# Remainders of the w_in and w_out weights from a DMA that adds, with deeper rings and another order

## The chip, the cores and the metric

The kernel runs on one core of a Trainium2 chip, in one launch. The metric is the device time of that launch in microseconds (us). The core has a matrix engine (TensorE, in the profile PE), a vector engine (VectorE, DVE), a scalar engine with tables (ScalarE, ACT), a general engine (GpSimd, POOL), a queue engine that here only issues DMAs (SyncE, SP), and 16 DMA engines, all of which can work on one transfer. Each engine takes its instructions in the order in which they stand in its queue.

## The reference

All arithmetic is float32. The first block is two layers of a transformer with modulation from a condition vector; the second block is two further layers with other mixers.

```python
def first_block(...):                      # DEPTH = 2; x: 512 tokens, h = ctx: 256 tokens, D_MODEL = 1024
    for l in range(DEPTH):
        mod = jnp.split(sc @ w_mod[l] + b_mod[l], 6, axis=-1)
        ...
        pc = hn @ w_in[l]                  # last layer: keys and values of the context only
        xn = rms_norm(x, g_norm1[l]) * (1 + scale1) + shift1
        p = xn @ w_in[l]
        ...
        attn = attend_query_blocks(q, ...)
        x_new = mixers_and_ffn(x, p, attn, ...)
        ...

def mixers_and_ffn(...):
    four = fourier_mixer(p[..., OFF_F:OFF_C], w_f)
    conv = conv_module(p[..., OFF_C:OFF_P], dw_w, dw_b, ln_g, ln_b, w_pw)   # 31 taps per channel
    pool = pool_mixer(p[..., OFF_P:], w_pl, pl_scale)                       # windows of 2, 4, 8, 16 tokens
    mix = jnp.concatenate([attn, four, conv, pool], axis=-1) @ w_o
    x = x + gate1 * mix
    xn = rms_norm(x, g2) * (1 + scale2) + shift2
    return x + gate2 * swiglu(xn, w_fi, w_fo)

def second_block(x, ...):
    for layer in range(DEPTH):
        u = rms_norm_2(h, pre_norm[layer])
        ...                                # layer 0: retention and a short convolution; layer 1: causal latent attention
        h = h + rms_norm_2(y, post_norm[layer])
```

`w_in` of the first block has 1536 columns, `w_out` (here `w_o`) is 1024 x 1024, the hidden width of the FFN is 2816.

## The kernel before

A float32 product is made of three matmuls with rounded operands (`mm3`, from line 1162): each weight w is split on the chip into a rounded part `wh` and a remainder `wl` = w - `wh`, each activation into a rounded part and a remainder, and the product is wh x xh + wh x xl + wl x xh. The split of a weight is `weights()` (line 1144): a tile `raw` of 128 x 1024 (512 KB) is loaded by a DMA on SyncE's queue, rounded into `wh` (a CAST on ScalarE or VectorE), and subtracted into `wl` (a TENSOR_TENSOR on VectorE). The three tiles stand in rings: four `raw`, three `wh`, three `wl`. A `raw` tile is free when the subtraction has read it; a `wh` and a `wl` when TensorE has. The activations lie transposed, features on the partitions, 512 tokens of x and 256 tokens of the context beside each other on the free axis.

The stages, in the order of the span: the norm and the first modulation (to about 40 us); the product with w_in in twelve blocks of 128 columns (`WIN_ORDER`, line 67: a and g of the convolution's gate, k, q, v, the pooling and Fourier inputs), between which the mixers of layer 0 run (to about 250 us); the product with w_out (to about 360); the FFN of layer 0 (to about 960); the same for layer 1 (mixers 960 to 1100, w_out to 1185, FFN to about 1560); then the two layers of the second block. In the mixing stages VectorE makes the convolution's taps (`cy` and `cz`, one multiply and add for each of 31 taps, `conv_taps`, line 1302), attention's row sums, and the weight remainders; ScalarE makes exponentials, copies and roundings; GpSimd has the additions of the pooling mixer alone (`pool_task`, line 1367, tiles `ps`). The modulation vectors (`md`) are matmuls on `raw` tiles too in layer 0's mixing stage (`mod_block`, line 1252), and on tiles `mraw` of their own later. The out products take each of the eight blocks of `w_out` once for every 256 tokens: 24 loads in layer 0, 16 in layer 1; in layer 0 and in layer 1 together 26 weights of w_in are loaded.

What sets the order: the whole program is recorded first (`Rec`), and a planner (`Rec.order`, line 748) gives every operation an engine and a place in that engine's queue. It works with a cost for each operation (`cost`, from line 582), penalties for engines (`PEN_*`), an order of steps (`STEPS`), offsets of priority for each mixer (`SHIFTS`) and the depths of the rings. `issue` (line 985) then writes the queues out, so all instructions have one line in the profile, L1001; tiles are told apart by their names. `wi` is the product with w_in, `wo` the one with w_out, `fa`, `fg` and `fo` the FFN, `y` and the like the second block.

Of the kernel before, what the change touches and what calls it, by code (L numbers as in the profile page):

```python
# [69 lines left out]
CFG = {0: {'CONV_AUX': 8,  # L70
     'LATE': -49000.0,
     'LATEM': 26000.0,
# [8 lines left out]
     'PEN_PE': (0, 150, None),  # L81
# [16 lines left out]
 1: {'CONV_AUX': 6,  # L98
# [4 lines left out]
     'PEN_CP': (0, 0, None),  # L103
     'PEN_CZ': (0, 0, None),
     'PEN_PE': (0, 0, None),
# [18 lines left out]
     'PEN_RND': (0, None, None),  # L124
     'PEN_SQ': (None, 0, None),
# [8 lines left out]
     'backlog': 0,  # L134
     'table_slack': 504.2099999999999,
     'urgent': 11068.417919999998},
 3: {'PEN_ADD': (0, None),
     'PEN_AFF': (0, 0, None),
     'PEN_CP': (0, 0, None),
# [15 lines left out]
     'backlog': 0,  # L155
     'table_slack': 338.9702987999999,
     'urgent': 86776.39649279998}}
SHIFTS = {'mla': 10000.0,
 'ret': 12000.0,
 (0, 'c', 'attn'): 7000.0,  # L160
 (0, 'c', 'conv'): 39000.0,
 (0, 'c', 'four'): 16000.0,
 (0, 'c', 'pool'): 43000.0,
 (0, 'c', 'taps'): -92000.0,
# [2111 lines left out]
```

## Time and profile before

| | |
|---|---|
| time, median of 3 runs | 2245.21 us (2242.07 to 2246.84) |
| profiled execution, its time | 2242.23 us |
| its span, first to last instruction | 2240.2 us |
| TensorE busy | 2134.7 us, 95% |
| VectorE busy | 1418.0 us, 63% |
| ScalarE busy | 866.7 us, 39% |
| GpSimd busy | 22.2 us, 1% |
| bytes moved by DMA | 258.44 MB |
| mean granted TensorE clock | 0.98 |

Busy times count compute instructions; an engine that issues a DMA is not counted as busy. The granted clock is the mean over a stretch of what TensorE was given, as a share of its full 2.4 GHz; its lower level is 1.2 GHz. The releaser of a wait is the instruction that a waiting engine's semaphore was last set by.

### The profile page before, as it was taken

How to read it: one execution, taken by the hardware profiler on the slowest of the kernel's cores; microseconds unless marked ns; L12 is line 12 of the kernel's file. 1: busy time of each engine (PE TensorE's matmuls, PEld its weight loads, DVE VectorE, ACT ScalarE, POOL GpSimd, SP SyncE). 2: the span in 40 equal slices, each digit the busy share in tenths (PEclk: the TensorE clock that was granted, in tenths of full speed). 3: DMA queues.
4: the chain of work that ended last, by engine and by line, in shares of the span. 5: the costliest groups of instructions: out<-in, count | busy, mean ns of one | idle time of the engine just before them, and what ended most of it. 6: DMA issues, size and time to landing. Idle time of an engine off the chain costs nothing.

```text
span 2240.2 us, 32559 instructions
## 1 busy us (share of the span) xinstructions
PE 2134.7 (95%) x12922; PEld 1845.7 (82%) x12922; DVE 1418.0 (63%) x2671; ACT 866.7 (39%) x1646; POOL 22.2 (1%) x35
## 2 busy tenths in 40 slices
PE   7799999999999999888899999999999999999997
PEld 3477799888888888777798888888888888989887
DVE  6998886332232232899984333459775685787996
ACT  6457754111212111664852212215341341435662
POOL 0001000000000000000100000000000000000000
PEclk9799999999999999998999999999999999999998
DMA  8225464222331423422043232335323224543223
GB/s 306 98 98 181 161 217 137 76 98 67 125 101 60 148 78 120 145 89 90 20 142 95 96 110 94 113 117 162 104 85 99 90 89 121 166 139 113 66 77 123
DMA packets 87176, 258.44 MB, mean 115 GB/s; under 512 B 10480, under 2 KB 18160, under 8 KB 87024
## 3 DMA queue, kind: packets, MB, share of 16 engines
q1 hardware_dynamic: 87024, 256.36, 35.7%
q8 instruction: 101, 1.65, 0.3%
q14 instruction: 51, 0.42, 0.1%
HBM read 249.24 MB, written 2.10 MB: 112 GB/s over the span
## 4 chain that ended last, share of the span: by engine, by line
PE 77%; DVE 14%; ACT 4%; DMA 2%; issue 2%; SPq 1%; DVEq 0%; ACTq 0%
PE fa L1001 14%; PE fg L1001 14%; PE fo L1001 13%; PE y L1001 5%; PE wi L1001 5%; PE wo L1001 4%; PE gt L1001 2%; PE egc L1001 2%; PE md L1001 2%; DVE wl L1001 2%; PE ecb L1001 2%; PE ecx L1001 2%; PE ecc L1001 2%; PE egr L1001 2%; DVE cy L1001 1%
## 5 line engine op out<-in xcount | busy, mean ns | idle before, releaser
L1001 DVE TENSOR_TENSOR wl<-raw,wh 128x1024 fp32r<-128x1024 f32 (+5 forms) x387 | 434.6, 1125 | 41.4 <-ACT wh L1001 28.9
L1001 ACT CAST wh<-raw 128x1024 fp32r<-128x1024 f32 (+4 forms) x224 | 216.7, 970 | 417.4 <-PE fo L1001 197.4
L1001 DVE CAST wh<-raw 128x1024 fp32r<-128x1024 f32 (+4 forms) x163 | 105.3, 646 | 211.8 <-PE fa L1001 73.7
L1001 DVE TENSOR_TENSOR ft<-ft,fg 128x256 f32<-128x256 f32 (+1 forms) x66 | 39.4, 598 | 270.7 <-PE fg L1001 270.7
L1001 PE MATMUL fo<-hh,wl 128*128 128x512 f32 (+1 forms) x448 | 156.5, 349 | 6.7 <-DVE wl L1001 6.7
L1001 PE MATMUL fo<-hh,wh 128*128 128x512 f32 (+1 forms) x448 | 157.8, 352 | 0.0
L1001 PE MATMUL fo<-hl,wh 128*128 128x512 f32 (+1 forms) x448 | 157.2, 351 | 0.0
L1001 PE MATMUL fa<-yxh,wh 128*128 128x512 f32 (+1 forms) x384 | 144.9, 377 | 0.0
L1001 PE MATMUL fg<-yxh,wh 128*128 128x512 f32 (+1 forms) x384 | 144.4, 376 | 0.0
L1001 PE MATMUL fa<-yxl,wh 128*128 128x512 f32 (+1 forms) x384 | 143.9, 375 | 0.2 <-DVE yxl L1001 0.2
L1001 PE MATMUL fg<-yxl,wh 128*128 128x512 f32 (+1 forms) x384 | 143.9, 375 | 0.0
L1001 PE MATMUL fa<-yxh,wl 128*128 128x512 f32 (+1 forms) x384 | 142.8, 372 | 0.0
L1001 PE MATMUL fg<-yxh,wl 128*128 128x512 f32 (+1 forms) x384 | 142.7, 372 | 0.0
L1001 PE MATMUL y<-mxh,wl 128*128 128x256 f32 x384 | 110.9, 289 | 6.1 <-DVE wl L1001 6.1
L1001 PE MATMUL y<-mxh,wh 128*128 128x256 f32 x384 | 111.8, 291 | 4.7 <-DVE wh L1001 3.3
L1001 PE MATMUL y<-mxl,wh 128*128 128x256 f32 x384 | 110.1, 287 | 0.3 <-DVE mxl L1001 0.3
L1001 ACT ACTIVATE ft<-fa 128x256 f32<-128x256 f32 (+1 forms) x66 | 34.2, 526 | 178.1 <-PE fa L1001 178.1
L1001 PEld LDWEIGHTS fo<-hh,wl 128*128 128x128 f32 x448 | 85.9, 192 | 18.6 <-DVE wl L1001 7.1
L1001 PEld LDWEIGHTS fo<-hh,wh 128*128 128x128 f32 x448 | 85.4, 191 | 8.4 <-issue 1.7
L1001 PE MATMUL wi<-xxh,wh 128*128 128x512 f32 (+1 forms) x240 | 90.5, 377 | 1.6 <-DVE c L1001 0.7
L1001 PE MATMUL wi<-xxh,wl 128*128 128x512 f32 (+1 forms) x240 | 86.5, 360 | 5.3 <-DVE wl L1001 5.3
L1001 PEld LDWEIGHTS fo<-hl,wh 128*128 128x128 f32 x448 | 86.3, 193 | 5.6
(457 smaller groups left out, 5910.5 us busy)
## 6 DMA issues: line engine op xcount, KB each, us to landing
raw<-in_w SPq DMA_DIRECT2D x291, 512.0 KB, 3.6
mraw<-in_wm SPq DMA_DIRECT2D x48, 512.0 KB, 4.8
raw<-in_wm SPq DMA_DIRECT2D x32, 512.0 KB, 4.8
raw<-in_w SPq DMA_DIRECT2D x24, 448.0 KB, 3.4
raw<-in_w SPq DMA_DIRECT2D x32, 320.0 KB, 3.1
mraw<-in_wm SPq DMA_DIRECT2D x32, 256.0 KB, 5.9
raw<-in_w SPq DMA_DIRECT2D x16, 384.0 KB, 3.1
rw<-rt SPq DMA_DIRECT2D x76, 64.0 KB, 2.0
```

Source lines behind the costliest of these rows:

```text
L1001: getattr(engs[o.eng], method)(*[real(a) for a in args], **{k: real(v) for k, v in kw.items()})
```

## The change

For the weights whose key begins with `in` or `out` in layers 0 and 1 of the first block, 26 and 40 of them, the subtraction on VectorE goes. ScalarE instead writes `wl` = -`wh` (an ACTIVATE with Copy and scale -1), and a DMA issued from GpSimd's queue adds the `raw` tile to `wl` in place. `raw` is free when that DMA has landed. The rings become five `raw`, four `wh` and four `wl`; the space comes from a smaller scratch area for DMA descriptors and from tile sizes rounded up to a common size. The planner gets a cost for the new DMA and other settings: some of the penalties, about half of the offsets, the order of steps in both layers of the second block, and WOE and WOS, by which two w_out blocks rather than three are started early, over six rather than seven of the eight inputs.

```diff
-CFG = {0: {'CONV_AUX': 8,
+CFG = {0: {'ADD': ('in', 'out'),
+     'CONV_AUX': 8,
...
-     'WOE': 3,
+     'WOE': 2,
...
-     'WOS': 7,
+     'WOS': 6,
...
- (0, 'c', 'taps'): -92000.0,
+ (0, 'c', 'taps'): -112000.0,
...
+            if eng == "gpsimd":
+                return 1100.0, 1900.0 + (ap.p1 - ap.p0) * ap.n * 4 / 200.0, False
             return max(250.0, (ap.p1 - ap.p0) * ap.n * 4 / 332.0), 1900.0, False
...
-        h = self.pw.tile([P, 1024], F32R, tag="wh", bufs=3, name=self.name("wh"))
-        lo = self.pw.tile([P, 1024], F32R, tag="wl", bufs=3, name=self.name("wl"))
+        h = self.pw.tile([P, 1024], F32R, tag="wh", bufs=4, name=self.name("wh"))
+        lo = self.pw.tile([P, 1024], F32R, tag="wl", bufs=4, name=self.name("wl"))
         self.rnd(h[:, :n], t[:, :n], self.PEN_WH)
-        self.sub_l(lo[:, :n], t[:, :n], h[:, :n], self.PEN_WL)
+        if key[0] in self.ADD:
+            self.nc.scalar.activation(lo[:, :n], h[:, :n].bitcast(F32), AF.Copy, scale=-1.0)
+            self.nc.gpsimd.dma_start(out=lo[:, :n].bitcast(F32), in_=t[:, :n], accum_op=ALU.add)
+        else:
+            self.sub_l(lo[:, :n], t[:, :n], h[:, :n], self.PEN_WL)
...
-    NA, NB, NRAW = 53, 11, 4
+    NA, NB, NRAW = 53, 11, 5
...
-    nc = _bacc.Bacc("TRN2", target_bir_lowering=False, num_devices=1)
+    nc = _bacc.Bacc("TRN2", target_bir_lowering=False, num_devices=1, dynamic_dma_scratch_size=2048)
```

The settings of the second block are tables; in the order of the whole program VectorE has 2593 rows where it had 2650, ScalarE 1624 where it had 1557, GpSimd 100 where it had 34; ScalarE's table loads go from 46 to 49, TensorE's matmuls of 256 columns from 7274 to 7130 and those of 512 from 4746 to 4818.

GpSimd's queue up to the middle of layer 0's mixing stage stands like this in the kernel before, from its first pooling addition (`ps` is a partial window sum, `pb` the padded input):

```order
L1001 TENSOR_TENSOR ps_749<-pb_88 128x527
L1001 TENSOR_TENSOR ps_758<-ps_749 64x512
L1001 TENSOR_TENSOR ps_1802<-pb_96 128x527
L1001 TENSOR_TENSOR ps_1839<-ps_1802 128x525
L1001 TENSOR_TENSOR ps_1802<-ps_1839 128x520
L1001 TENSOR_TENSOR ps_1839<-ps_1802 64x512
```

and like this in the changed kernel, where the first five adds stand ahead of the first pooling addition:

```order
L1004 DMA wl_247<-raw_205 128x1024
L1004 DMA wl_265<-raw_221 128x1024
L1004 DMA wl_641<-raw_516 128x1024
L1004 DMA wl_674<-raw_538 128x1024
L1004 DMA wl_717<-raw_566 128x1024
L1004 ISA
L1004 TENSOR_TENSOR ps_802<-pb_91 128x527
L1004 TENSOR_TENSOR ps_815<-ps_802 64x512
L1004 DMA wl_841<-raw_799 128x1024
L1004 DMA wl_938<-raw_898 128x1024
L1004 DMA wl_1111<-raw_1054 128x1024
L1004 DMA wl_1233<-raw_1173 128x1024
```

The adds are now between the pooling additions, in one queue.

On VectorE the remainders of the k, q and later weights stand behind the taps of the convolution in the kernel before:

```order
L1001 SCALAR_TENSOR_TENSOR cy_702<-cb_693,spt,cy_702 128x505
L1001 SCALAR_TENSOR_TENSOR cy_940<-cb_928,spt,cy_940 128x253
L1001 TENSOR_TENSOR cy_702<-cy_702,cz_751 128x504
L1001 SCALAR_TENSOR_TENSOR cy_940<-cb_928,spt,cy_940 128x252
L1001 TENSOR_REDUCE modT_303<-md_148_974 128x8
L1001 TENSOR_TENSOR wl_1058<-raw_936,wh_983 128x1024
L1001 SCALAR_TENSOR_TENSOR cy_940<-cb_928,spt,cy_940 128x251
L1001 TENSOR_TENSOR modT_303<-modT_303,spt 128x8
L1001 TENSOR_TENSOR wl_1068<-raw_956,wh_994 128x1024
L1001 SCALAR_TENSOR_TENSOR cy_940<-cb_928,spt,cy_940 128x250
```

In the changed kernel these subtractions are gone from VectorE, and ScalarE has the rounding and the negated copy of the first of those weights one behind the other:

```order
L1004 COPY pb_91<-wi_691 128x512
L1004 COPY pb_88<-wi_702 128x256
L1004 COPY ps_815<-ps_802 64x512
L1004 CAST wh_828<-raw_799 128x1024
L1004 ACTIVATE wl_841<-wh_828 128x1024
L1004 CAST wh_928<-raw_898 128x1024
L1004 ACTIVATE wl_938<-wh_928 128x1024
L1004 ACTIVATE sg_942<-wi_874 128x256
L1004 ACTIVATE sg_946<-wi_869 128x512
```

The copy `wl` follows its `wh` directly, ahead of the gate (`sg`) and the taps (`cz`) of the convolution's second 128 channels.

On TensorE the end of the fourth block of the w_in product (`wi`) is followed in the kernel before by two modulation blocks (`md`) and a piece of the context's layer norm (`cm`), and then by the next block:

```order
L1001 MATMUL wi_856<-xc_600,wl_786 128x256
L1001 MATMUL md_922<-raw_574,scp 32x512 x2
L1001 MATMUL md_922<-raw_609,scp 32x512 x2
L1001 MATMUL cm_932<-cy_709,cst 128x256
L1001 MATMUL md_922<-raw_780,scp 32x512 x2
L1001 MATMUL md_922<-raw_796,scp 32x512 x2
L1001 MATMUL md_148_974<-cst,mrow_966 128x128 x4
L1001 MATMUL md_1006<-raw_972,scp 32x512 x2
L1001 MATMUL md_1006<-raw_987,scp 32x512 x2
L1001 MATMUL md_1006<-raw_1016,scp 32x512 x2
L1001 MATMUL md_1006<-raw_1021,scp 32x512 x2
L1001 MATMUL md_155_1041<-cst,mrow_1038 128x128 x4
```

In the changed kernel the next block, with `wh_828` and `wl_841`, comes between the parts of the first modulation block:

```order
L1004 MATMUL wi_874<-xc_601,wl_717 128x256
L1004 MATMUL md_948<-raw_579,scp 32x512 x2
L1004 MATMUL md_948<-raw_596,scp 32x512 x2
L1004 MATMUL wi_959<-xxh_324,wh_828 128x512
L1004 MATMUL wi_959<-xxl_328,wh_828 128x512
L1004 MATMUL wi_959<-xxh_324,wl_841 128x512
L1004 MATMUL md_948<-raw_695,scp 32x512 x2
L1004 MATMUL md_948<-raw_761,scp 32x512 x2
L1004 MATMUL wi_959<-xxh_326,wh_828 128x512
L1004 MATMUL wi_959<-xxl_333,wh_828 128x512
L1004 MATMUL wi_959<-xxh_326,wl_841 128x512
L1004 MATMUL wi_1001<-xc_370,wh_828 128x256 x2
```

The block of the w_in product has moved ahead of most of the modulation work.

## Rows read from the trace of the kernel before

**Rows 1.** The page: busy time, share of the span, instructions of each engine.

```profile
PE 2134.7 (95%) x12922; PEld 1845.7 (82%) x12922; DVE 1418.0 (63%) x2671; ACT 866.7 (39%) x1646; POOL 22.2 (1%) x35
```

**Rows 2.** Windows: length, busy time of each engine, granted clock, DMA share, GB/s.

```profile
30.00:64.00 34.00, 33.31 (x198) 24.20 (x190) 24.12 (x69) 28.32 (x64) 0.66 (x1) 1.00 0.62 225
64.00:120.00 56.00, 41.33 (x182) 28.07 (x182) 54.13 (x108) 17.12 (x30) 1.57 (x2) 0.76 0.36 122
120.00:250.00 130.00, 121.25 (x734) 96.67 (x733) 112.63 (x269) 92.05 (x189) 11.09 (x12) 0.96 0.41 133
250.00:360.00 110.00, 107.42 (x849) 96.21 (x848) 94.76 (x195) 68.06 (x133) 0.00 (x0) 1.00 0.65 215
...
960.00:1100.00 140.00, 120.25 (x727) 104.68 (x727) 131.57 (x242) 92.19 (x163) 7.91 (x6) 0.93 0.20 63
1100.00:1185.00 85.00, 82.16 (x661) 79.80 (x661) 73.22 (x148) 55.32 (x112) 0.00 (x0) 1.00 0.33 102
```

**Rows 3.** Chain of waits, 45 to 130 us: start, length, what.

```profile
67.01 1.15 DVE wl L1001
...
94.03 14.10 DVE cy L1001 x28
...
109.14 1.15 DVE wl L1001
```

**Rows 4.** Timeline, ScalarE: start, length, instruction.

```profile
92.84 1.03 ACT L1001 CAST wh<-raw 128x1024 fp32r<-128x1024 f32 x1
```

**Rows 5.** Timeline, VectorE, the same stretch.

```profile
109.06 1.22 DVE L1001 TENSOR_TENSOR wl<-raw,wh 128x1024 fp32r<-128x1024 f32 x1
```

**Rows 6.** Waits of TensorE, 60 to 120 us: total, times, longest.

```profile
PE wi L1001 <- DVE wl L1001: 5.3, 2, 4.1
PE md L1001 <- DVE cy L1001: 3.7, 1, 3.7
```

**Rows 7.** Waits of TensorE, 960 to 1100 us.

```profile
PE qss L1001 <- ACT qsq L1001: 5.7, 1, 5.7
PE cm L1001 <- DVE cy L1001: 4.8, 2, 3.9
```

**Rows 8.** Tile wl on VectorE, 64 to 250 us: count, durations in ns, first and last.

```profile
L1001 DVE TENSOR_TENSOR wl<-raw,wh x10: 1205/1217/1223, 66.9 to 205.0; 128x1024 fp32r<-128x1024 f32 x10
```

**Rows 9.** The same, 960 to 1060 us.

```profile
L1001 DVE TENSOR_TENSOR wl<-raw,wh x12: 1212/1218/1226, 967.6 to 1050.2; 128x1024 fp32r<-128x1024 f32 x12
```

**Rows 10.** Groups by line and shape, VectorE: busy us, mean ns, idle before.

```profile
L1001 DVE TENSOR_TENSOR wl<-raw,wh 128x1024 fp32r<-128x1024 f32 x291 | 354.7, 1221 | 17.0 <-ACT wh L1001 5.6 <-DVE wh L1001 0.5
```

**Rows 11.** The same, ScalarE.

```profile
L1001 ACT CAST wh<-raw 128x1024 fp32r<-128x1024 f32 x162 | 169.5, 1049 | 280.1 <-PE fo L1001 102.2 <-PE fg L1001 100.5 <-PE wi L1001 15.4
L1001 ACT ACT_TABLE_LOAD x46 | 59.0, 1283 | 2.4 <-PEq L2265 0.7 <-DVE rp L1001 0.6 <-PE r L1001 0.4
```

**Rows 12.** Tile ps on GpSimd, whole span.

```profile
L1001 POOL TENSOR_TENSOR ps<-pb x6: 638/1104/1948, 63.3 to 1077.5; 128x527 f32<-128x527 f32 x4, 128x271 f32<-128x271 f32 x2
```

**Rows 13.** DMA, 250 to 360 us: queue, packets, MB, share; issues, KB, landing.

```profile
q1 hardware_dynamic: 6471, 23.56, 64.1%
...
raw<-in_w SPq DMA_DIRECT2D x29, 512.0 KB, 4.4
```

**Rows 14.** Tile wo on TensorE, 250 to 360 us, one form of three.

```profile
L1001 PE MATMUL wo<-mxh,wh x128: 278/283/467, 298.9 to 357.5; 128*128 128x256 f32 x128
```

**Rows 15.** The page: copies within SBUF, KB each, us to landing.

```profile
rw<-rt SPq DMA_DIRECT2D x76, 64.0 KB, 2.0
```

**Rows 16.** Waits of TensorE, 900 to 960 us.

```profile
PE fo L1001 <- DVE wl L1001: 8.1, 2, 4.3
```

**Rows 17.** Waits of TensorE, 1500 to 2240 us.

```profile
PE y L1001 <- DVE wl L1001: 6.1, 4, 2.2
PE y L1001 <- DVE wh L1001: 3.3, 2, 1.6
PE fo L1001 <- DVE wl L1001: 3.0, 1, 3.0
```

More of the change, by code (lines that the diff above doesn't have):

```diff
@@ L67 @@
 WIN_ORDER = ["a0", "g0", "a1", "g1", "k", "qA", "qB", "v", "p0", "p1", "f0", "f1"]
-CFG = {0: {'CONV_AUX': 8,
+CFG = {0: {'ADD': ('in', 'out'),
+     'CONV_AUX': 8,
      'LATE': -49000.0,
-     'LATEM': 26000.0,
+     'LATEM': 25000.0,
      'LATEW': -3000.0,
@@ L80 @@
      'PEN_CZ': (0, 0, None),
-     'PEN_PE': (0, 150, None),
+     'PEN_PE': (0, 0, None),
      'PEN_RND': (0, None, None),
@@ L97 @@
      'urgent': 3873.946271999999},
- 1: {'CONV_AUX': 6,
+ 1: {'ADD': ('in', 'out'),
+     'CONV_AUX': 6,
      'FOC': 5000.0,
@@ L102 @@
      'PEN_CA': (0, None),
-     'PEN_CP': (0, 0, None),
+     'PEN_CP': (300, 0, None),
      'PEN_CZ': (0, 0, None),
-     'PEN_PE': (0, 0, None),
+     'PEN_PE': (0, 300, None),
      'PEN_RND': (0, 1000, None),
@@ L123 @@
      'PEN_PE': (0, 0, None),
-     'PEN_RND': (0, None, None),
-     'PEN_SQ': (None, 0, None),
+     'PEN_RND': (0, 150, None),
+     'PEN_SQ': (300, 0, None),
      'PEN_SUB': (0, None),
@@ L128 @@
      'PEN_WL': (0, None),
[5 rows of a table removed]
-     'backlog': 0,
-     'table_slack': 504.2099999999999,
-     'urgent': 11068.417919999998},
[5 rows of a table added]
+     'backlog': 1.5,
+     'table_slack': 2722.7339999999995,
+     'urgent': 29884.72838399999},
  3: {'PEN_ADD': (0, None),
-     'PEN_AFF': (0, 0, None),
-     'PEN_CP': (0, 0, None),
+     'PEN_AFF': (0, 300, None),
+     'PEN_CP': (0, 300, None),
      'PEN_PE': (0, 0, None),
@@ L145 @@
      'PEN_WL': (0, None),
[7 rows of a table removed]
[6 rows of a table added]
      'YE': 1,
      'YS': 4,
-     'backlog': 0,
+     'backlog': 0.25,
      'table_slack': 338.9702987999999,
@@ L158 @@
 SHIFTS = {'mla': 10000.0,
- 'ret': 12000.0,
+ 'ret': -8000.0,
  (0, 'c', 'attn'): 7000.0,
- (0, 'c', 'conv'): 39000.0,
- (0, 'c', 'four'): 16000.0,
+ (0, 'c', 'conv'): 42000.0,
+ (0, 'c', 'four'): 11000.0,
  (0, 'c', 'pool'): 43000.0,
- (0, 'c', 'taps'): -92000.0,
+ (0, 'c', 'taps'): -112000.0,
  (0, 'x', 'attn'): -3000.0,
- (0, 'x', 'conv'): 48000.0,
+ (0, 'x', 'conv'): 56000.0,
  (0, 'x', 'four'): 19000.0,
@@ L171 @@
  (1, 'x', 'conv'): 63000.0,
- (1, 'x', 'four'): -6000.0,
- (1, 'x', 'pool'): 84000.0,
+ (1, 'x', 'four'): -3000.0,
+ (1, 'x', 'pool'): 83000.0,
  (1, 'x', 'taps'): 25000.0}
@@ L971, in order @@
                     finish(o, end)
-                    heapq.heappush(events, (end + (o.lat if e == "sync" else 0.0) + FREE, 1, o.idx))
+                    heapq.heappush(events, (end + (o.lat if e in ("sync", "gpsimd") else 0.0) + FREE, 1, o.idx))
                     heapq.heappush(events, (end, 2, -1))
@@ L1018 @@
     PTW = 4
+    ADD = ()
     PEN_RND = (0.0, None, None)
@@ L1097, in W @@
     def W(self, n, nm="w"):
-        return self.A(nm=nm) if n <= 512 else self.pp.tile([P, n], F32, tag="w", bufs=4, name=self.name(nm))
+        return self.A(nm=nm) if n <= 512 else self.pp.tile([P, 544], F32, tag="w", bufs=4, name=self.name(nm))[:, :n]
     def two(self, n, nm, mk=None):
@@ L1874, in first_layer @@
         self.ffn(l, groups, after)
-    NA, NB, NRAW = 53, 11, 4
+    NA, NB, NRAW = 53, 11, 5
     def setup(self):
         nc = self.nc
-        t = self.psm.tile([P, 8, 2], F32, tag="sc", bufs=1, name="sc")
+        t = self.ptop.tile([P, 24], F32, name="sc")[:, :16].rearrange("p (k v) -> p k v", v=2)
         nc.scalar.activation(t, self.S("c").rearrange("p (k v) -> p k v", v=2), AF.Silu)
@@ L2225, in run @@
             nsp = sum(n for _, n in self.sp_at.values())
-            self.spt = pc.tile([P, nsp], F32, name="spt")
+            self.spt = pc.tile([P, nsp + 40], F32, name="spt")[:, :nsp]
             self.scp = pc.tile([P, 8, 32], F32, name="scp")
@@ L2239, in run @@
             self.nph = 0
+            self.ptop = pool("top", bufs=1, side="right")
             self.pm = pool("pm", bufs=4, space=PSUM, reuse_waits="tile")
```

23 rows, old and new, of the table CFG are left out of this document.

## The prediction

> **What bounds the kernel now.** I first read the page: TensorE is busy 95% of the span, VectorE 63%, ScalarE 39%, GpSimd 1% [rows 1]. So the kernel can only get shorter where TensorE idles or runs at its lower clock. I then cut the span into stages with the windows view and looked, in each row, at TensorE's busy time against the length, at which other engine is nearly full, at the granted clock and at the DMA share [rows 2]. 30 to 64 us is full (33.31 of 34). The mixing stage of layer 0, 64 to 250 us, leaves TensorE 14.67 + 8.75 = 23.4 us idle, while VectorE is busy 54.13 + 112.63 = 166.8 of 186 us, 90%. The mixing stage of layer 1, 960 to 1100 us, leaves 19.75 us idle with VectorE at 131.57 of 140, 94%. The stages of the w_out product, 250 to 360 and 1100 to 1185 us, leave only 2.6 and 2.8 us, and the first has the DMA engines at a mean share of 0.65.
>
> Third, the chain of waits in the first mixing stage: a subtract `wl` of 1.15 us releases TensorE at 68.2, a run of convolution taps `cy` of 14.1 us follows at 94.0, and behind it stands another `wl` at 109.14 [rows 3]. The timeline says why: ScalarE had rounded a `wh` at 92.84, yet the subtract that was next starts on VectorE only at 109.06, behind the taps [rows 4, 5]. The waits of TensorE there are 5.3 us on `wl` and 3.7 on `cy` [rows 6]. In layer 1 the longest is on ScalarE's `qsq`, 5.7 us, and then on the taps, 4.8 [rows 7]: VectorE is full, but the last to arrive is not always a weight.
>
> **The change, part by part.** The sum is made against the profiled execution, 2242.2 us; the median of the runs is 2245.2, 3.0 higher.
>
> 1. Subtracts leave VectorE in the mixing stages. Ten subtracts of 128x1024 stand between 64 and 250 us [rows 8], each 1.22 us busy [rows 10] and 1.15 us in the chain [rows 3]. Removed: 10 x 1.15 = 11.5 us of an engine that is 90% full. To that I add part of TensorE's 4.1 us wait at 68.2, which ends with the subtract: behind a DMA that is fed by ScalarE the weight no longer queues with taps. The orders shown above agree: the negated copy stands right behind its rounding on ScalarE, no tap between, and TensorE's next w_in block comes ahead of most of the modulation work. I take 15 us. From below, 0: the taps are then next on VectorE's queue and the same wait is for them. From above 23.4, all of the idle time; at a mean clock of 0.76 and 0.96 [rows 2] another 0.24 x 56 + 0.04 x 130 = 18.6 could come back, if TensorE idled no longer ahead of its slow stretches, so the far bound is 42. In layer 1 twelve leave [rows 9]: 12 x 1.15 = 13.8; since the longest wait there is ScalarE's I take 12, bounds 0 and 19.75 + 0.07 x 140 = 29.6.
>
> 2. What takes their place. Each of the 66 weights (26 of w_in, 40 of w_out) now has a negated copy on ScalarE and a DMA on GpSimd's queue. The copy has the shape of the cast `wh` on ScalarE, 1.05 us [rows 11], together 66 x 1.05 = 69 us. ScalarE is busy 92 of 130 and 92 of 140 us in the mixing stages [rows 2], so the copies lie beside other work, with VectorE as the cover; were it gone, 22 of them (those two stages) cost up to 23 us. The order has three more ACT_TABLE_LOADs, 3 x 1.28 = 3.8 [rows 11]. I take +3, bounds 0 and +27. On GpSimd's queue the adds stand with the additions of the pooling mixer in one order, and the first of these waits for the pooled input: an add behind it waits too, and behind the add the loads of the raw ring on SyncE. One pooling addition is 0.64 to 1.95 us [rows 12], so one that stands ahead of an add and has its input costs it at most 2 us, which is in the bounds.
>
> 3. The w_out stages. Here the subtracts cost nothing (the idle time of the first is 2.6 us with TensorE 98% busy), so the gain is at most 2.6 and what is added can only lose. In 250 to 360 us the DMA engines are busy 64.1% of the time, 70.5 us, for 23.56 MB [rows 13], which makes 0.524 / 23.56 x 70.5 = 1.57 us of all 16 for one weight. 24 adds now come on top. The trace has no such operation. From below: like a load of the same bytes, 24 x 1.57 = 37.7, and 70.5 + 37.7 = 108.2 of 110 us, which just fits. From above: both operands cost as much as a load, 24 x 3.14 = 75.4, 145.9 us of DMA in 110, +36. I take +10, nearer to the first, which it equals in bytes written; the loads ahead of the stage can be brought earlier, but DMA slices that stand idle in between cannot all be filled. The raw ring: one weight of the second half takes TensorE 3.7 us (128 matmuls of each of three forms, 24 in all per weight, so 16 weights, from 298.9 to 357.5 [rows 14]), and five raw tiles cover 18.4 us. A tile is held 4.4 us for the load [rows 13], 1.05 for the cast, 1.05 for the copy, about 1 to 2 for GpSimd and then for the landing of the add, for which the nearest row is a copy within SBUF of 64 KB, 2.0 us [rows 15]; with 1.57 for the bytes 4 us, with twice the bytes 6. That is 11 to 15 us: the ring holds. In layer 1 the share is 0.33 of 85 us = 28, and 16 adds bring 25 to 50: 53 to 78 of 85. I take +2 for the longer way of each first weight, bounds -2.8 and +10.
>
> The Trainium skill speaks against the change here ("Collectives: The Full Stack", section "The bandwidth ceiling: the fold count and why AG ≠ RS ≠ AR"): a DMA that adds reads two sources, and so moves about half of what a copy does. By that rule the add stands at my upper bound, and the sum would be that of case A; no row of before shows an add.
>
> 4. Deeper rings and the new order. Over the rest TensorE waits 8.1 us on `wl` between 900 and 960 us and 6.1, 3.3 and 3.0 us on `wl`, `wh` and `wl` after 1500 [rows 16, 17]: 20.5 us. A fourth `wh`/`wl` and a fifth raw tile let one weight more be ready. But these waits name VectorE, which works off its own queue, and the subtracts of these weights stay there; a deeper ring helps only where the load or the slot came late. I take a quarter, -5, bounds 0 and -20.5.
>
> 5. At nothing: the aligned tiles, the smaller scratch and the setup tile (same instructions, same shapes); the merged steps of the retention layer (144 matmuls of 256 columns become 72 of 512: same columns); WOE and WOS (two w_out blocks started early instead of three, in a stage where TensorE hardly waits); the five adds ahead of 64 us, where TensorE is full and VectorE is busy 24 of 34 us. If that cover is gone, each is late by one add's 4 to 6 us, and the stage's first weights are in use by then.
>
> Sum: -15 - 12 + 3 + 10 + 2 - 5 = **-17**. 2242.2 - 17 = 2225.2, and 3.0 for the median: **2228**.
>
> **The rivals.**
> A, slower: the adds fill the DMA engines in layer 0's w_out stage. For it: the share of 0.65 and a mean way of 4.4 us per load already [rows 13]. Against it: in layer 1 there is room, and loads can come ahead. At 3.14 us per add, +36 and +5: -15 - 12 + 3 + 36 + 5 - 5 = +12, **2257**. It decides from the price at which the stage gives back the other 17 + 10 us: (110 + 27 - 70.5) / 24 = 2.8 us of the 16 engines per add.
> B, no gain: the mixing stages don't follow VectorE; the taps, `qsq` and the attention's chain on ScalarE, which now has 23 us more, arrive last. For it: in the layer 1 stage no `wl` is among the longest waits [rows 7]. A third of the 27, -9, then +3 + 10 + 2 - 5: +1, **2246**.
> C, more: both mixing stages lose their whole idle time and the adds fit in one pass: -23.4 - 19.75 - 5 + 3 + 0 = -45, **2200**. For it: the chain passes through `wl` at both ends of the stall from 88 to 110 us [rows 3]; against it, the order of VectorE keeps the taps.
> D, the adds are late wherever VectorE is busy. For it: of six first additions of the pooling mixer on GpSimd the median is 1.1 us and the longest 1.95, with four of the six of one shape [rows 12], so something holds that engine up at times. If its work on the DMAs stretches as much, the weights of the mixing stages land later, half of the 27 is lost: -13.5 + 3 + 10 + 2 - 5 = -3.5, **2242**. The Trainium skill has a rule of this kind ("SBUF — State Buffer", section "SBUF: two separate sides"): while VectorE runs certain copies, GpSimd cannot write the descriptors of its DMAs. No row here shows a descriptor being written.
>
> **How the numbers follow.** The forecast has 0.50, its own range 2212 to 2240 (one of the terms half way to its bound on either side); C 0.16, A 0.16, B 0.13, D 0.05. A measurement tells about 0.2%, 4.5 us, from no change, so same is 2240.7 to 2249.7. Faster: 0.50 + 0.16 = 0.66. Same: B and D, 0.18. Slower: A, 0.16. The range from 2200 to 2257 leaves out the better half of C and the worse half of A, 0.16.
>
> **What would show it.** Step 1: in 64 to 120 us VectorE's busy time falls by some 5 us and TensorE's waits on `wl` go; the span from the first w_in matmul to the first w_out matmul is 12 to 20 us shorter. Wrong if TensorE then waits as long on `cy` or on the adds. Step 2: the negated copies at 1.05 us each; an add 4 to 6 us from issue to landing; GpSimd's queue waiting for raw landings and copies, not the other way round. Step 3: a DMA share over 0.9 in layer 0's w_out stage and TensorE waiting there for `wl` by about 10 us; at a share of 1.0 with 30 us or more of waits it is A, at 0.9 or less without waits the add is cheaper than I hold. Step 4: the 8.1 us before the second FFN product and those after 1500 us smaller by a quarter. An add that lands after 10 us or more would break the ring's account and make the whole wrong.

## The result, and the profile after

The changed kernel takes 2296.14 us (median of 4 runs, 2289.77 to 2299.32), the kernel before 2244.47 beside it: a ratio of 1.0227, interval 1.0202 to 1.0252. It is 2.3% slower, where 2228 was forecast. In what follows one run of e1 (9165 us), two of e2 (2994 and 4202) and one of the kernel before beside them (4195) ran far slower than the others of the same kernel and are left out of the medians. The profiled execution took 2295.56 us, its span is 2293.8 us.

The first lines of the page answer to [rows 1]; under them stand the queue of the adds in the list of DMA queues (packets, MB, share of the 16 engines over the span) and the add in the list of issues (KB each, median us to landing):

```profile
PE 2150.5 (94%) x12850; PEld 1847.1 (81%) x12850; DVE 1342.8 (59%) x2612; ACT 925.5 (40%) x1704; POOL 77.8 (3%) x101
...
q0 software_dynamic: 9504, 34.61, 7.9%
...
wl<-raw POOLq DMA_DIRECT2D x66, 512.0 KB, 6.4
```

VectorE has lost 75 us of work and ScalarE has 59 more, the way the change moves it. The new queue took 7.9% of 16 engines over 2293.8 us: 181 us, or 2.75 us of all 16 engines for each of the 66 adds.

The windows of the same stretches as [rows 2]:

```profile
30.00:64.00 34.00, 27.92 (x155) 18.71 (x156) 18.85 (x56) 27.07 (x58) 1.72 (x2) 1.00 0.85 283
64.00:120.00 56.00, 52.76 (x299) 41.60 (x298) 55.87 (x124) 35.01 (x61) 6.96 (x7) 1.00 0.66 186
120.00:250.00 130.00, 118.62 (x767) 93.64 (x767) 113.94 (x278) 97.72 (x199) 14.41 (x16) 0.99 0.60 186
250.00:360.00 110.00, 91.46 (x630) 76.29 (x629) 57.74 (x148) 59.98 (x101) 17.04 (x20) 0.89 0.91 249
...
960.00:1100.00 140.00, 118.60 (x700) 103.47 (x699) 113.78 (x220) 99.33 (x163) 15.99 (x18) 0.91 0.57 138
1100.00:1185.00 85.00, 57.94 (x305) 47.79 (x304) 42.73 (x95) 43.20 (x78) 5.80 (x5) 0.70 0.05 13
```

The first mixing stretch did what was hoped: 64 to 120 us has TensorE busy for 52.76 us where it was 41.33, at a granted clock of 1.00 where it was 0.76. The loss lies mainly in two places. From 250 to 360 us the DMA share is 0.91 (0.65 before) and TensorE idles 18.5 us; and from 1100 to 1185 us TensorE is busy for 57.94 of 85 us at a clock of 0.70, with the DMA engines at a share of 0.05, so next to nothing was being loaded there. A smaller loss stands ahead of both: from 30 to 64 us TensorE is busy for 27.92 us where it was 33.31, and 4.2 us of that are waits for the first adds:

```profile
PE wi L1004 <- DMA wl<-raw: 4.2, 2, 2.6
```

To compare kernels whose stages slide against each other, the trace of each was cut at the start of the last matmul of a stage: the last `wo` of layer 0, the last `fo` of layer 0, the last `wo` and `fo` of layer 1, the last `y`. The lengths between these cuts, in us (the end after the last `y` is 12 to 14 us in all), are those of the profiled execution of each kernel; e1 to e14 are the experiments below:

| kernel | layer 0 to its last wo | FFN 0 | layer 1, mixing and w_out | FFN 1 | second block | span |
|---|---|---|---|---|---|---|
| before | 357.8 | 598.0 | 210.6 | 370.0 | 691.3 | 2240.2 |
| after | 379.1 | 588.1 | 275.2 | 361.3 | 677.4 | 2293.8 |
| e1, no adds | 342.7 | 597.9 | 205.7 | 363.7 | 676.6 | 2199.3 |
| e2, copy for add | 359.1 | 589.5 | 255.8 | 361.3 | 677.3 | 2255.7 |
| e3, GpSimd subtracts | 398.5 | 588.9 | 298.4 | 361.2 | 676.5 | 2336.4 |
| e4, pooling early | 384.5 | 587.9 | 225.0 | 363.4 | 675.7 | 2249.2 |
| e5, rings alone | 349.7 | 598.7 | 208.1 | 365.6 | 688.8 | 2223.3 |
| e6, settings alone | 360.4 | 597.8 | 218.5 | 370.4 | 695.5 | 2256.2 |
| e7, w_in of layer 0 | 334.2 | 598.5 | 204.7 | 363.7 | 676.8 | 2190.6 |
| e8, w_out | 382.0 | 589.8 | 223.0 | 362.1 | 677.3 | 2246.9 |
| e9, w_in of both | 333.7 | 600.2 | 239.9 | 364.1 | 676.7 | 2227.3 |
| e10, rings and adds | 387.3 | 590.9 | 242.1 | 360.9 | 688.3 | 2282.0 |
| e11, third of w_out | 360.1 | 593.1 | 203.5 | 363.7 | 676.6 | 2209.7 |
| e12, not the first | 346.2 | 601.2 | 203.6 | 363.7 | 677.9 | 2205.3 |
| e13, w_in, pooling early | 336.2 | 598.3 | 214.0 | 363.7 | 675.8 | 2200.7 |
| e14, rings, w_in of layer 0 | 346.6 | 595.6 | 206.9 | 365.6 | 687.6 | 2214.8 |

Against before, after loses 21.3 us to the end of layer 0's w_out stage and 64.6 in layer 1, and gains 9.9, 8.7 and 13.9 elsewhere.

In layer 0's w_out stage, from 228 to 380 us, the DMA view (queue, packets, MB, share; then issues, KB, median us to landing) answers to [rows 13]; the share of the two queues together is 87%:

```profile
q1 hardware_dynamic: 6799, 24.78, 46.3%
q0 software_dynamic: 3312, 12.06, 40.7%
...
raw<-in_w SPq DMA_DIRECT2D x31, 512.0 KB, 5.8
wl<-raw POOLq DMA_DIRECT2D x23, 512.0 KB, 8.6
mraw<-in_wm SPq DMA_DIRECT2D x14, 512.0 KB, 8.2
```

23 adds took 40.7% of 152 us, 2.69 us of all 16 engines each. They land 8.6 us after their issue, and the loads take longer too: 5.8 us for a raw tile where it was 4.4. The waits of SyncE's queue in the same window (total, times, longest) and of TensorE:

```profile
SPq L1004 <- DMA wl<-raw: 88.6, 22, 10.5
SPq L1004 <- PE md L1004: 34.5, 10, 11.3
```

```profile
PE md L1004 <- DMA mraw<-in_wm: 13.3, 6, 4.7
PE wo L1004 <- DMA wl<-raw: 5.0, 4, 1.6
```

SyncE, which issues every load, stood 88.6 us waiting for adds to land so that a raw tile came free. In the kernel before it stood 41.9 us waiting for subtracts, from 250 to 360 us:

```profile
SPq L1001 <- DVE wl L1001: 41.9, 15, 6.9
```

The modulation's loads (tiles `mraw`) stand in the same queue, and TensorE's longest waits are for these, 13.3 us, not for a remainder, 5.0 us.

In layer 1 the picture is another. The window between the last early w_out matmul and the next one:

```profile
1123.00:1178.00 55.00, 30.91 (x128) 23.20 (x126) 18.76 (x42) 19.53 (x36) 0.00 (x0) 0.59 0.00 0
```

For 55 us no DMA moves. GpSimd's timeline, and ScalarE's at the end of that stretch (start, length, instruction, idle before it and its releaser):

```profile
1100.67 0.89 POOL L1004 DMA_DIRECT2D wl<-raw  x1 [7.94 <-PE sc L1004]
...
1185.88 1.81 POOL L1004 DMA_DIRECT2D wl<-raw  x2 [78.55 <-ACT wl L1004]
```

```profile
1178.10 0.69 ACT L1004 ACTIVATE pt<-po,spt 128x512 f32<-128x512 f32 x1 [1.36 <-PE po L1004]
...
1183.51 1.04 ACT L1004 CAST wh<-raw 128x1024 fp32r<-128x1024 f32 x1 [4.08 <-PE wo L1004]
1184.46 3.89 ACT L1004 ACTIVATE wl<-wh 128x1024 fp32r<-128x1024 f32 x4
```

GpSimd's next add stands behind 78.55 us of idle time, which a negated copy ends. That copy is behind a rounding `wh` which waits for TensorE to free one of the four `wh` tiles, and TensorE frees none: every w_out group of the first 256 tokens needs the pooling mixer's second half as its last input, for which ScalarE's copy starts only at 1178.10. The product `po` of that half stands on TensorE's queue behind all of attention, though its inputs lay ready from 1121.4 on, when VectorE finished the second of them (`pll`, started at 1120.72). So attention ran alone, with TensorE busy for 30.91 of 55 us at a granted clock of 0.59, near the lower of its two levels.

### The profile page after: what moved, and what is told of

Its sections match the earlier page's. It is cut to its first block, busy times and chain, and to the rows that moved or that the text cites. A ratio compares the mean times of both kernels' runs of the same rounds, so it can differ in the third digit from the quotient of the medians.

```text
span 2293.8 us, 32626 instructions
## 1 busy us (share of the span) xinstructions
PE 2150.5 (94%) x12850; PEld 1847.1 (81%) x12850; DVE 1342.8 (59%) x2612; ACT 925.5 (40%) x1704; POOL 77.8 (3%) x101
## 4 chain that ended last, share of the span: by engine, by line
PE 73%; DVE 10%; DMA 7%; ACT 5%; issue 4%; SPq 1%; POOL 0%; DVEq 0%; POOLq 0%; ACTq 0%
PE fa L1004 13%; PE fg L1004 13%; PE fo L1004 12%; PE y L1004 5%; DMA wl<-raw 3%; PE wi L1004 3%; DVE cy L1004 2%; PE wo L1004 2%; PE gt L1004 2%; PE egc L1004 2%; PE ecb L1004 2%; PE ecc L1004 2%; PE md L1004 2%; PE egr L1004 2%; PE ecx L1004 2%
## 5 line engine op out<-in xcount | busy, mean ns | idle before, releaser
L1004 DVE TENSOR_TENSOR wl<-raw,wh 128x1024 fp32r<-128x1024 f32 (+6 forms) x319 | 351.4, 1104 | 51.1 <-ACT wh L1004 42.2
L1004 ACT CAST wh<-raw 128x1024 fp32r<-128x1024 f32 (+5 forms) x234 | 223.4, 960 | 312.6 <-PE fo L1004 160.6
L1004 DVE CAST wh<-raw 128x1024 fp32r<-128x1024 f32 (+4 forms) x151 | 98.8, 656 | 231.2 <-PE fa L1004 52.1
L1004 PE MATMUL wo<-mxh,wl 128*128 128x256 f32 x256 | 77.9, 304 | 13.2 <-DMA wl<-raw 13.1
```

What stands on the lines that cost most here:

```text
L1004: getattr(engs[o.eng], method)(*[real(a) for a in args], **{k: real(v) for k, v in kw.items()})
```

## The experiments

e5, e10 and e14 start from the kernel before, all others from the changed kernel. Each was compared with the kernel before on its own chip (medians there 2241.9 to 2243.1 us). Wherever an edit changes what the planner sees, it makes a new order, so that two kernels seldom differ in the edit alone; only e2 and e3 keep the changed kernel's order.

**e1: what the rest of the change does without adds.**

```diff
-CFG = {0: {'ADD': ('in', 'out'),
+CFG = {0: {'ADD': (),
...
- 1: {'ADD': ('in', 'out'),
+ 1: {'ADD': (),
```

> The changed kernel with every remainder subtracted on VectorE again (ADD empty); rings of 5, 4 and 4, the aligned tiles and the new settings stay, and the planner makes a new order. Theory (the adds cost it: 2.7 us of all 16 DMA engines each in layer 0's w_out stage, and in layer 1's the order that was made with them): 2225 to 2250 us, the w_out stage of layer 0 about 103 us and that of layer 1 about 75 us. Rival (the settings and rings cost it): 2280 us or more, with layer 1's w_out stage still above 100 us.

2200.01 us, ratio 0.9797 (0.9765 to 0.9829): below the range of the theory, and the rival fails. Rings, tiles and settings gain 2%; the adds, with the order that they bring, turn this into a loss of 2.3%, 96 us between the two.

**e2: the second operand alone.**

```diff
-            self.nc.gpsimd.dma_start(out=lo[:, :n].bitcast(F32), in_=t[:, :n], accum_op=ALU.add)
+            self.nc.gpsimd.dma_start(out=lo[:, :n].bitcast(F32), in_=t[:, :n])
```

> The changed kernel, same order, with the DMA on GpSimd's queue writing the raw tile over wl instead of adding it: the subtraction is left out for these 66 weights, and the second operand is not read. Theory (the add's price is its second operand): a transfer takes about 1.6 us of the 16 engines instead of 2.75, lands in 4 to 5 us instead of 8.6 in layer 0's w_out stage, that stage shrinks from 149 us by some 25; layer 1's w_out stage stays long; in all about 2270 us. Rival (a DMA from GpSimd's queue is dear whatever it does): 2.7 us again, 2290 to 2300 us.

The DMA now only copies, so the remainders are not those of the reference. 2259.98 us, ratio 1.007 (1.0042 to 1.0097), 36 us under the changed kernel with the same order on every queue. In layer 0's w_out stage, 227 to 359 us, the queue of the copies, and GpSimd's group of issues (count, busy us, mean ns; idle before):

```profile
q0 software_dynamic: 3312, 12.06, 22.7%
...
wl<-raw POOLq DMA_DIRECT2D x23, 512.0 KB, 5.6
```

```profile
L1004 POOL DMA_DIRECT2D wl<-raw x66 | 36.3, 550 | 553.9 <-ACT wl L1004 361.1 <-PE wo L1004 78.7 <-ACT c L1004 19.6
```

22.7% of 132 us for 23 copies is 1.30 us of 16 engines each, where the add took 2.69: 2.07 times as much with the same 12.06 MB on the queue, which fits the reading of a second operand. The copy also takes GpSimd 0.55 us to issue, the add 0.86 (durations in ns: least, median, most):

```profile
L1004 POOL DMA_DIRECT2D wl<-raw x66: 859/862/1194, 23.1 to 1229.0; - x66
```

The stage ends 20 us earlier than with adds, but still 16 later than without any (e1). The second operand is a good half of the loss there; the rest is the way over a DMA, with its bytes, and the order made for it. The theory holds, with a copy somewhat cheaper than its 1.6 us, a stage shorter by 20 us instead of 25, and a total 10 us below its 2270; the rival fails.

**e3: a subtract on GpSimd for each add, the same order.**

```diff
                 for method, args, kw in o.calls:
+                    if o.eng == "scalar" and kw.get("scale") == -1.0:
+                        self.neg = args[1]
+                        self.negs[id(args[0].tile)] = args[1]
+                        continue
+                    if o.eng == "gpsimd" and method == "dma_start":
+                        h = self.negs[id(kw["out"].tile)]
+                        self.real.gpsimd.tensor_tensor(real(kw["out"].bitcast(F32R)), real(kw["in_"]), real(h), op=ALU.subtract)
+                        continue
```

> The changed kernel, the same order on every queue, with one TENSOR_TENSOR subtract on GpSimd in the place of each add and nothing in the place of the negated copy: no DMA is added. Theory: layer 0's w_out stage falls from 149 us to 105 to 120, DMA share 0.65; layer 1's stays over 100 us because its loss is in the order of TensorE's queue; in all 2250 to 2265 us. Rival (everything lost is lost to the adds on the DMA engines): 2235 to 2245 us, layer 1's stage about 75 us.

2334.38 us, ratio 1.0396 (1.0363 to 1.0429): both expectations missed. The subtract takes GpSimd 2.4 us, and VectorE's `sq` can last as long beside it. GpSimd's and VectorE's timelines, and the tile `sq` on VectorE in e3 and before:

```profile
308.20 2.40 POOL L1011 TENSOR_TENSOR wl<-raw,wh 128x1024 fp32r<-128x1024 f32 x1 [1.48 <-DVE wh L1013]
```

```profile
307.38 0.69 DVE L1013 CAST wh<-raw 128x1024 fp32r<-128x1024 f32 x1
...
308.49 2.39 DVE L1013 TENSOR_TENSOR sq<-ct 128x256 f32<-128x256 f32 x1
```

```profile
L1013 DVE TENSOR_TENSOR sq<-ct x4: 2110/2332/2386, 304.9 to 316.2; 128x256 f32<-128x256 f32 x4
```

```profile
L1001 DVE TENSOR_TENSOR sq<-ct x1: 426/426/426, 294.1 to 294.1; 128x256 f32<-128x256 f32 x1
```

The `sq` beside the GpSimd subtract lasts 2.39 us; the same operation took 0.43 in the kernel before. So this kernel brings a loss of its own and says nothing on the adds in layer 0. It does show layer 1's w_out stage still long with no add in it, which agrees with the order as the cause there, but a slowed VectorE lengthens that stage too.

**e4: the pooling product earlier.**

```diff
- (1, 'x', 'pool'): 83000.0,
+ (1, 'x', 'pool'): 43000.0,
```

> The changed kernel with one number of the settings, the offset of layer 1's pooling mixer, 43000 instead of 83000: up to layer 1's mixing stage the order is the same, then the second pooling product comes before the last eight score products of attention instead of after all of them. Theory (layer 1's w_out stage loses because the second pooling product stands behind attention, and all four wh and wl wait for it): the stretch of 1123 to 1178 us in which TensorE has attention alone goes, 30 to 45 us, 2250 to 2265 us in all. Rival (the adds themselves hold layer 1 up): 2285 us or more.

2250.36 us, ratio 1.003 (1.0012 to 1.0048), 46 us under the changed kernel by one number. Layer 1 took 225.0 us where it was 275.2; layer 0 is as without this edit within 6 us, though its order is the same, so lengths of this stage differ by that much between executions. The window of layer 1's w_out stage, with 12 of its 16 adds in it:

```profile
1114.00:1198.00 84.00, 74.91 (x568) 70.92 (x567) 55.14 (x129) 63.30 (x111) 11.01 (x12) 0.96 0.65 163
```

TensorE is busy for 74.9 of 84 us. The theory holds: nearly half of the 96 us lay in the place of one small product on TensorE's queue. Layer 1 stays 19 us longer than in e1.

**e5 and e6: rings and settings apart.** e5 is the kernel before with the rings, tiles and scratch of the change; e6 is e1 with the rings of before.

```diff
-        h = self.pw.tile([P, 1024], F32R, tag="wh", bufs=3, name=self.name("wh"))
-        lo = self.pw.tile([P, 1024], F32R, tag="wl", bufs=3, name=self.name("wl"))
+        h = self.pw.tile([P, 1024], F32R, tag="wh", bufs=4, name=self.name("wh"))
+        lo = self.pw.tile([P, 1024], F32R, tag="wl", bufs=4, name=self.name("wl"))
...
-    NA, NB, NRAW = 53, 11, 4
+    NA, NB, NRAW = 53, 11, 5
```

> The kernel before with the rings of 5, 4 and 4, the aligned tiles and the smaller scratch alone: no add, settings of before, and the planner makes a new order. Theory (of the 43 us that the changed kernel without adds gains, most comes from the settings; the rings give a quarter of TensorE's 20 us of waits on weights): 2230 to 2242 us. Rival (the rings carry it): 2200 to 2215 us.

> The changed kernel without adds and with the rings of before (4, 3 and 3): the settings alone. Theory (settings carry): 2205 to 2220 us. Rival (the rings carry it, or the settings need them): 2235 us or more.

e5: 2223.93 us, 0.9909 (0.9881 to 0.9938), between theory and rival. e6: 2259.17 us, 1.0071 (1.0046 to 1.0096). The rings (with their tiles and scratch) gain 19 us alone; the settings alone lose 16; together they gain 43. For e6 the rival was right: the settings need the rings. With the rings of before the second block is 4 us longer than before, with the deeper ones 15 shorter.

**e7: adds for layer 0's w_in alone.**

```diff
-CFG = {0: {'ADD': ('in', 'out'),
+CFG = {0: {'ADD': ('in',),
...
- 1: {'ADD': ('in', 'out'),
+ 1: {'ADD': (),
```

> The changed kernel with adds for the w_in weights of layer 0 alone, 13 of the 66; the w_out weights and layer 1 are subtracted on VectorE. Theory (the adds pay where VectorE is 90% busy and TensorE waits for remainders, and cost where the DMA engines are busy): layer 0's w_in product ends near 205 us instead of 212, the w_out stage is about 95 us as without adds, in all 2190 to 2200 us. Rival (what the mixing stage gains is given back before the w_out stage ends, since the attention's end sets it): 2198 to 2206 us.

2191.35 us, ratio 0.977 (0.9741 to 0.9798), in the theory's range: the fastest of all, 2.3% under the kernel before. It is 9 us under e1; the two intervals overlap, but the traces agree, with 8.5 us less to the end of layer 0's w_out stage and layer 1 and the rest the same within 1 us. TensorE's waits from 60 to 120 us, in e1 and in e7:

```profile
PE wi L1004 <- DVE wl L1004: 11.6, 1, 11.6
```

```profile
PE wi L1004 <- DMA wl<-raw: 2.6, 1, 2.6
```

The 11.6 us wait for a subtract behind the taps is gone, and 2.6 us of wait for an add has come (4.3 us from 30 to 230 us).

**e8: adds for w_out alone.** The edit is `'ADD': ('out',)` in both layers.

> The changed kernel with adds for the 40 w_out weights alone. Theory: the DMA engines' share in layer 0's w_out stage is 0.85 to 0.92, the stage is 35 to 45 us longer than without adds, layer 1's 5 to 15 us longer where its order isn't spoiled, in all 2240 to 2260 us. Rival (the w_in adds ahead of the stage delay its loads): below 2225 us.

2250.81 us, ratio 1.003 (1.0012 to 1.0049), in the theory's range and 51 us over e1. Layer 0 ends 39 us later than in e1 and its FFN gives 8 back; layer 1 is 17 us longer. From 246 to 382 us the adds' queue has 47.8%, 2.83 us of all 16 engines for each of 23.

**e9 and e13: adds for w_in in both layers,** the second with the pooling offset of e4.

```diff
-CFG = {0: {'ADD': ('in', 'out'),
+CFG = {0: {'ADD': ('in',),
...
- 1: {'ADD': ('in', 'out'),
+ 1: {'ADD': ('in',),
...
- (1, 'x', 'pool'): 83000.0,
+ (1, 'x', 'pool'): 43000.0,
```

> The changed kernel with adds for the w_in weights of both layers, 26 of the 66. Up to layer 1's mixing stage it should be e7_w_in_layer0. Theory (in layer 1 the last to arrive is ScalarE's chain and the taps, not the remainders; the adds bring ScalarE 13 copies and put 2.7 us of DMA time each ahead of the small rotation copies): layer 1's w_in product takes longer than the 94 us of e7, by 5 to 20 us, in all 2195 to 2215 us. Rival (VectorE at 94% sets that stage too): 2176 to 2188 us.

> e9_w_in_both (adds for w_in of both layers) with the offset of layer 1's pooling mixer at 43000, which puts the second pooling product two groups of score products earlier. Theory (two losses in layer 1: the w_in product is 112 us with adds instead of 94, and the w_out stage waits for the late pooling product): the first stays, the second goes: 2204 to 2216 us. Rival (all of it is the place of the pooling product): 2188 to 2196 us. Second rival (none of it is): 2222 to 2230 us.

e9: 2227.04 us, 0.9933 (0.9918 to 0.9948), worse than its theory and its rival. e13: 2203.45 us, 0.983 (0.9814 to 0.9847), half a microsecond under the lower end of its theory; both rivals fail. Layer 1 is 35 us longer than in e7 with the late pooling product, 9 with the early one. In layer 1 these adds bring no gain in either. That the 9 us are the adds' own is not shown: e7 with the early offset was not run, and in e13 the last `po` still has 8 of layer 1's 64 score matmuls behind it, where e7 has 40. One candidate for what the adds cost is the small copies of the rotation of k and q (`rw`). Who waited for them, and their landing (min, median, max), over layer 1's mixing, in e7 and in e9:

```profile
DVE rw L1004: 0.6, 2
...
DMA to landing us min/median/max: 1.9/2.0/3.1
```

```profile
DVE rw L1004: 6.6, 3
...
DMA to landing us min/median/max: 2.0/3.6/5.1
```

They lie in the chain of k and q, and beside adds of 512 KB the median is 1.6 us longer; in e13 it is 2.4 us, and VectorE waited 6.8 us for them. The waits are 6 us longer in both, out of 35 and 9.

**e10: all adds under the old settings.** e5 with `'ADD': ('in', 'out')` in both layers and the code of the change for it.

> The kernel before with the deeper rings and with all 66 adds, settings of before. Theory (an add costs what it costs, whatever the settings): beside e5_rings_only (2224 us) layer 0's w_out stage is some 40 us longer with a DMA share near 0.9, the whole 2260 to 2300 us. Rival (the new settings fit the adds badly): 2235 us or less.

2281.07 us, ratio 1.0168 (1.0151 to 1.0186), in the theory's range, 57 us over e5. Layer 0 ends 38 us later, layer 1 takes 34 longer. In layer 0 the adds cost the same with either settings, 36 to 39 us; in layer 1 they cost 34 us with these and 70 with the new ones.

**e11: nine of the 24 adds in layer 0's w_out stage.**

```diff
-        if key[0] in self.ADD:
+        if key[0] in self.ADD or key in (('out', 0, 0), ('out', 0, 3), ('out', 0, 6)):
```

> e7_w_in_layer0 with adds for three of the eight w_out blocks of layer 0 as well, 9 of the 24 loads. Theory (the DMA engines are the limit of that stage: 0.55 of 100 us without adds, and 9 x 2.7 = 24 us more fit): share 0.75 to 0.8, stage within 5 us of e7's 104, 2188 to 2198 us. Rival (each add costs its longer way, with the raw tile held, whatever the share): 9/24 of 40 us, 15 us longer, 2203 to 2210 us.

2209.24 us, ratio 0.9856 (0.9841 to 0.9871): in the rival's range, 18 us over e7. The window from 234 to 360 us has a DMA share of 0.72, so on average the engines have room:

```profile
234.00:360.00 126.00, 116.42 (x876) 104.32 (x876) 91.69 (x200) 75.80 (x141) 7.33 (x10) 0.96 0.72 220
```

The same for the w_out stage of e7:

```profile
230.00:334.00 104.00, 104.00 (x829) 96.69 (x825) 95.81 (x197) 73.94 (x140) 0.00 (x0) 1.00 0.55 196
```

The chain of waits, 255 to 362 us, shows where the time went:

```profile
273.98 9.37 DMA wl<-raw
...
312.44 11.31 DMA wl<-raw
...
347.02 7.86 DMA wl<-raw
```

Three adds lie in the chain with 9.4, 11.3 and 7.9 us from issue to landing. A subtract has 1.2 us in that place. TensorE idles 9.6 us of this window, where e7 has it busy throughout, and its granted clock is 0.96 where e7 has 1.00. While these three adds were on their way the share was 0.88, 0.92 and 0.86, and the shortest landing of an add in the changed kernel was 4.4 us. So a stage with room on average loses all the same; whether an add alone, without loads beside it, would have cost this is not shown.

**e12: without the first three blocks.**

```diff
-        if key[0] in self.ADD:
+        if key[0] in self.ADD and key[2] not in ('a0', 'g0', 'p0'):
```

> e7_w_in_layer0 with the first three blocks of layer 0's w_in (a0, g0, p0), of whose weights TensorE waits 4.0 us for adds before 70 us, subtracted on VectorE: 10 adds. Theory: those waits go and nothing else changes much, 2186 to 2191 us. Rival (VectorE, freed earlier, was worth more, or the new order loses it): 2192 to 2200 us.

2205.14 us, ratio 0.9834 (0.9819 to 0.9849): above the range of the theory and of the rival. The waits for adds are gone from 30 to 130 us (0.2 us), but others have come, the longest of 5.8 us for the modulation's `modT`, and the last w_in matmul starts at 218.1 us where e7 has 206.7. This agrees with the rival's second half, an order that loses the gain; what in the order does it was not tested.

**e14: the add in layer 0's w_in under the old settings.** e5 with `'ADD': ('in',)` in layer 0.

> e5_rings_only (settings of before, deeper rings) with adds for layer 0's 13 w_in weights. Theory (the add pays in that stage whatever the settings): the w_in product ends 5 to 9 us earlier than e5's 213.9, in all 2213 to 2220 us against e5's 2224. Rival (the gain hangs on the settings that were made with the adds): 2224 us or more.

2217.7 us, ratio 0.9892 (0.9877 to 0.9906), in the theory's range and 6 us under e5. The intervals of the two overlap, so with the old settings a gain is likely rather than shown, and it is not where the theory put it: w_in ends only 0.6 us earlier than in e5; 3 us come by the end of the w_out stage and 3 in the FFN.

## Why the prediction was wrong

The sign was wrong, by two terms, that of layer 0's w_out stage (step 3) and that of the order in layer 1, which was not in the sum (step 2); the rings and the settings (steps 4 and 5), taken too small, hid part of it.

**Step 1, subtracts that leave the mixing stages.** In layer 0 the mechanism was right and the size too large: 15 us were forecast, e7 against e1 shows 8.5 at the end of the stage. The wait that I read in the chain, for a subtract behind the taps at about 109 us, was the one that went. My sign for it did not come: VectorE's busy time from 64 to 120 us was 55.87 us instead of 54.13, with 124 instructions instead of 108: other work took the place of the subtracts. In layer 1 the term failed: -12 was forecast and e13 against e7 shows +9, with part of the order in it. I had written that the longest wait there is ScalarE's and took nine tenths of the subtracts all the same. In e13 VectorE is busy 9 us less from the start of layer 1 to the end of its w_out stage than in e7, and TensorE gained nothing from that; during layer 1's w_in product it waited longest for ScalarE's `qsq` in e7, 6.7 us, and for adds in e13, 4.5 us. What makes up the +9 was not taken apart; the slower rotation copies are one candidate. The bound of 0 did not hold either, since I let the adds cost that stage nothing but ScalarE's time.

**Step 2, what takes their place.** The counts were right. The groups on ScalarE (count, busy us, mean ns), beside [rows 11]:

```profile
L1004 ACT ACTIVATE wl<-wh 128x1024 fp32r<-128x1024 f32 x66 | 69.3, 1057 | 40.4 <-DVE wh L1004 30.6 <-PE wo L1004 5.8 <-issue 3.5
L1004 ACT ACT_TABLE_LOAD x49 | 62.9, 1283 | 1.6 <-PEq L2275 0.7
```

1.06 us for a negated copy and 49 table loads, as forecast. I asked what the add waits for behind the pooling additions, but not what the planner would move because of that: in the order of the changed kernel the last pooling product `po` of layer 1 stands behind the last score product `sc` on TensorE, where before three groups of score products, 12 of layer 1's 64 score matmuls, stood behind it. The offset of that mixer had only gone from 84000 to 83000; without adds the same settings put 40 behind it (e1), adds for w_out alone 20 (e8), and none stand there in e9 and e10, which like the changed kernel have adds for layer 1's w_in. The place could be read without any time. It cost 46 us (e4).

**Step 3, the w_out stages.** The term failed that was taken as +10, between 0 and +36. The add cost 2.69 us of the 16 engines (2.83 in e8), between my ends of 1.57 and 3.14 and next to the price of 2.8 at which case A decides. I took the lower end because the add writes as many bytes as a load. The rule of the Trainium skill that stood beside it ("Collectives: The Full Stack", section "The bandwidth ceiling: the fold count and why AG ≠ RS ≠ AR") is that an add reads two sources and so runs at about half the rate of a copy, there in a collective. The runs agree, outside one: 1.30 us for e2's copy, 2.69 for the add. Case A put the stage at +36, at 3.14 us per add; it was +36.4 against e1 and +39.3 in e8. That the numbers agree so well is partly luck, since the price was lower and the mechanism of A is only part of it. I had the landing at 4 to 6 us and the raw ring as safe up to 10; the median in the stage was 8.6, the longest in the kernel 13.2, and SyncE waited 88.6 us for it. By my own account of the ring a tile was then held for 5.8 us of load, 1.05 of cast, 1.06 of copy, 0.86 of issue and 8.6 of way, an estimate of 17.4 us before any waiting between them, against the 18.4 that five tiles cover: nothing was left. The sign that I had set, TensorE waiting for `wl`, came small, 5.0 us; it waited more for `mraw`, which the same queue loads. e11 shows that nine adds, at a mean share of 0.72, already cost 26 us of that stage's end. How the rest divides between full engines and the long way was not taken apart further. The planner, whose price for the add is in the diff, 1.9 us and 512 KB at 200 bytes per ns, 4.5 us in all, worked with a landing that the stage did not have. For layer 1's w_out stage +2 was forecast with +10 as the bound; e8 shows +17 for layer 1, and the late pooling product came on top.

**Step 4, deeper rings.** -5 was forecast, bounds 0 and -20.5; e5 shows -19. I argued that waits that name VectorE are not helped by a slot. Of the 20.5 us of waits that I had counted 11.4 are left in e5, so the quarter was too small; and a new one of 3.2 us on `wl` has come, for `eq`. The span is 16.9 us shorter, 8 of them by the end of layer 0's w_out stage, where I had counted no wait for the rings, and the rest in layer 1 and the second block. That the ring decides how early a weight can be loaded and split, and so what the planner can place where, is argued; no run shows it by itself.

**Step 5, at nothing.** The settings were put down at nothing and are worth -24 with the new rings (e1 against e5) and +16 with the old (e6). The second block alone is 12 us shorter in e1 than in e5. I had looked at the merged columns alone, not at the order of the steps. The five adds ahead of 64 us were at nothing too, and TensorE waited 4.2 us for them; e12, without three of them, is no faster for it.

**The rivals.** A named the right place; its price of 3.14 us was above the measured 2.69, and its 2257 us misses layer 1. B's doubt, that the mixing stages don't follow VectorE, fits layer 1, where taking subtracts from VectorE gained nothing. D's price had no sign: GpSimd issued an add in 859 to 1194 ns, median 862, and VectorE's `sq` (median) 418 ns where it was 419.

Without the adds the forecast of the rest would have been far too small; with them it had the wrong sign. The best kernel here, e7, keeps 13 of the 66 adds, and its gain of 2.3% is mostly that of the rings and settings, 2% (e1).

## What to carry to other kernels

A DMA that adds trades 1.2 us of VectorE for 2.7 us of all DMA engines and 6 to 9 us of way, in which the source tile stays taken. It also takes 1.06 us of ScalarE. In these kernels that paid in one place, layer 0's w_in product, where TensorE really waited for a subtract, which one wait in the chain shows better than a busy share; it lost where the DMA engines had loads to bring, and room on average did not save it (e11). Where a planner writes the queues, look in its new order for small operations that have moved behind a long chain, at the last input of each product that holds ring slots, before summing durations; and change ring depths and settings in separate kernels, since each can hide what the other is worth.

## What the runs showed of the hardware

An accumulating DMA within SBUF of 512 KB took 2.69 to 2.83 us of all 16 engines (the changed kernel, e8), a plain one from the same queue 1.30; GpSimd spent 0.86 and 0.55 us on the issue. Small copies of 64 KB landed after 2.4 to 3.6 us (median; e13, e9) beside such adds instead of 2.0 (e7). And while GpSimd ran a subtract of two SBUF tiles for 2.4 us, an operation of VectorE with SBUF operands that takes 0.43 us alone lasted 2.11 to 2.39 (e3).
